# Down projections of a two-layer trunk: twelve instead of ten of 22 k-blocks in block products, the tiles reordered, square sums by transfers

## The chip, the cores and the metric

The kernel runs on one core of one Trainium2 chip. The metric is the device time of one execution in microseconds. TensorE (PE) multiplies matrices, VectorE (DVE) and ScalarE (ACT) do the elementwise work, SyncE (SP) and GpSimd (POOL) issue transfers; POOL also issues the transfers that add into their destination. Each engine runs its instructions in order and waits on semaphores for the others.

## The reference

Two layers over 512 positions of width 1024, float32. Layer 0 mixes with pooling and a gated short convolution, layer 1 with gated linear attention; each is followed by a gated convolution FFN of width 2816, and a final norm ends the trunk. The change concerns the last product of the FFN, `@ w_down`, and the sums of squares for the norms that follow it:

```
def rmsnorm(x, g):
    xf = x.astype(jnp.float32)
    y = xf * lax.rsqrt(jnp.mean(xf * xf, axis=-1, keepdims=True) + EPS)
    return (y * g.astype(jnp.float32)).astype(x.dtype)

def conv_ffn(h, w_up, conv_w, conv_b, w_down):
    u, v = jnp.split(h @ w_up, 2, axis=-1)
    u = causal_dwconv(u, conv_w, conv_b)
    return (jax.nn.gelu(u, approximate=False) * v) @ w_down

for l in range(DEPTH):
    ...
    x = x + y
    x = x + conv_ffn(rmsnorm(x, ffn_norm[l]), ffn_w_up[l], ffn_conv_w[l], ffn_conv_b[l], ffn_w_down[l])
return rmsnorm(x, final_norm)
```

## The kernel before

Channels lie on the 128 partitions, the 512 positions along a row. A float32 operand is split into a high part (rounded to the fast matmul type, by ScalarE) and a low part (the rest, by VectorE); every product is three passes: high by high, high by low, low by high.

**Down projection.** The 2816 inner channels are 22 k-blocks of 128, the output is eight tiles of 128 channels. Of the k-blocks, `NPLAIN` = 12 are multiplied plainly (`down`, two blocks of weights per tile as `DOWN_K` says). The other 10 are used in a scheme of Strassen and Winograd: the outputs are taken in four pairs of tiles (2p, 2p+1), the ten k-blocks as `HD` = 5 left and 5 right ones, the positions as two halves. In place of eight block products of 128 channels by 5 k-blocks by 256 positions there are seven, p1 to p7 (`DOWN_SEVEN` is their order), on sums of weights and sums of activations. `mix_m` forms and splits the activation sums for one left and one right k-block, HD times a layer; `down_seven` issues a pair's products and adds their results.

**Weights of a pair.** Four of the five k-blocks come by `seven_weights`. SP loads the left half (`raw 0`) and the right part (`raw 1`). The tile `s31` (tag "sum", `sums` buffers) is loaded by SP with a block twice over and then gets two more blocks added by a transfer that POOL issues (`add_sum`). From these VectorE makes s2 (`s2_sum`, L500, which reads s31 and raw 0) and s4 (`s4_sum`); ScalarE and VectorE split the pieces a1, s31p, s2 and a2 (L489, L495). The fifth k-block comes by `extra_weights`: three loads into `raw_e`, three VectorE sums (L548 to L550), one split (hi_e, lo_e). p1 and p2 use a1, p6 uses s2, p5 and p7 use s31p, p3 and p4 use a2; `seven_product` appends the extra block to each pass.

**Order.** Every step of TensorE, VectorE and ScalarE is entered with `at(t, ...)` and a planned time; `run_plan` sorts the entries and issues them, so each of these engines works in exactly that order. SP's and POOL's transfers are issued as their buffers and sources allow. The times `when` and `begin` in `seven_weights` are relative to the first product of the pair. Raw weights have three buffers (`wp`), split weights four of each kind (`wsp`), PSUM eight banks. The `dn` stage holds the "sum" buffers (two) and small ones.

Four whole plain tiles and tile 4 come first, then half of tile 5; behind each of the first three pairs stands one plain half tile, behind the last pair the whole of tile 7. After a pair, `done_left` and `done_right` add its tiles to x (`add_left`, `add_right`, `add_x`) and call `finish`, which squares the tile on ScalarE and adds it into a sum on VectorE (`square_acc`, L299). In the last layer tile 7 is done in two halves of positions, and `last` scales the first half and sends it out while the second is computed: `part` and `root` make the norm, `spread_small` spreads it, `scale_first` multiplies two tiles and sends them; `after(n, ...)` counts matmuls.

Of the kernel before, what the change touches and what calls it, by code (L numbers as in the profile page):

```python
# [14 lines left out]
P = 128  # L15
# [46 lines left out]
DOWN_LEFT = [NPLAIN + i for i in range(HK)] + [NF - 2]  # L62
DOWN_RIGHT = [NPLAIN + HK + i for i in range(HK)] + [NF - 1]
NDOWN = 6

COLS = {}
# [13 lines left out]
def trunk_kernel(ctx, tc, xT, cols, w_first, w_lead, w_ab, w_pool, w_abo, w_vg, w_qk, w_r, w_g2, w_go, w_up, w_dn, w_ds, w_de, out):  # L80
# [211 lines left out]

    def square_acc(k, acc, ts=slice(0, T)):
        if k == 0 and ts.start == 0:
            S.activation(acc[:, ts], x[0][:, ts], AF.Square)
            return
        sq = slot(name="sq")
        S.activation(sq[:, ts], x[k][:, ts], AF.Square)
        V.tensor_tensor(acc[:, ts], acc[:, ts], sq[:, ts], ALU.add)  # L299

# [160 lines left out]
    def seven_weights(src, base, pool, sums, behind=False, lead=None, later=0.0, begin=(26.0, 20.0, 15.4, 9.7), early=0.0):  # L461
# [73 lines left out]
    def extra_weights(src, base):  # L535

        e = {}

        def load():
            e["raw"] = wp.tile([P, WBLK], F32, tag="raw", name="raw_e")[:, : 7 * P]  # L540
            nc.sync.dma_start(e["raw"][:, : 2 * P], src[:, : 2 * P])
            e["r"] = e["raw"].rearrange("p (a n) -> p a n", n=P)
            nc.sync.dma_start(e["r"][:, 2:4, :], src[:, None, 2 * P : 3 * P].broadcast_to([P, 2, P]))
            nc.sync.dma_start(e["r"][:, 6, :], src[:, 3 * P :])

        def sums():
            r = e["r"]
            V.tensor_tensor(r[:, 2:4, :], r[:, 2:4, :], r[:, 0:7:6, :], ALU.add)  # L548
# [3 lines left out]
        def high():  # L552
            e["hi"] = wsp.tile([P, WPITCH], F32R, tag="hi", name="hi_e")[:, SKEW : SKEW + 7 * P]
            S.activation(e["hi"], e["raw"], AF.Copy)

        def low():
            e["lo"] = wsp.tile([P, WPITCH], F32R, tag="lo", name="lo_e")[:, SKEW : SKEW + 7 * P]
            V.tensor_tensor(e["lo"], e["raw"], f32(e["hi"]), ALU.subtract)

        at(base - 12.0, load)  # L560
        at(base - 7.0, sums)
        at(base - 3.0, high)
        at(base - 1.7, low)
        return e

    def seven_product(w, b, ops, name, out, first, ts, only=None, low_last=False, extra=None):
        if out not in b:
            b[out] = bank("st" + out)
        piece, side = LEFT[name]
        ks = [slice(side * QUARTER + k * P, side * QUARTER + (k + 1) * P) for k in range(HK)]  # L570
        h, lo = [[t[:, c] for c in ks] for t in w[piece]]
        if extra:
            c = (EXTRA_AT[piece] + side) * P
            h, lo = h + [extra["hi"][:, c : c + P]], lo + [extra["lo"][:, c : c + P]]
        ah, al = ops[name]()
        for i in range(3) if only is None else (only,):
            wt, a = ((h, ah), (lo, ah), (h, al))[i] if low_last else ((h, ah), (h, al), (lo, ah))[i]
            for k in range(len(a)):
                PE.matmul(  # L579
                    b[out][:, ts], wt[k], a[k],  # L580
                    start=first and i == 0 and k == 0, stop=i == 2 and k == len(a) - 1,
                    skip_group_check=True,
                )
# [73 lines left out]
    def ffn(l, acc, mixed, finish, ahead, halves_last=False):  # L657
# [223 lines left out]
        def plain_down(j, n=None):  # L881
            nonlocal t
            while blocks and n != 0 and (blocks[0][0] == j or (j == 0 and blocks[0][0] < 4)):
                jj, k0, kt = blocks.pop(0)
                n = n and n - 1
                first = t < base + 9.5 * UNIT
                block(t - 16.0, t - (9.3 if first else 6.0), t - (7.0 if first else 4.5))
# [11 lines left out]

        def done_left(p, late=0.0):  # L900
            at(t + late + 0.3, lambda: add_left(p))
            at(t + late + 2.3, lambda: finish(2 * p))

        def done_right(p, t):
            at(t, lambda: add_right(p))
            at(t + 2.4, lambda: finish(2 * p + 1))

        plain_down(0)
        plain_down(4)
        plain_down(5, 1)  # L910
        for p, (j, n) in enumerate(((5, 1), (6, 1), (6, 1), (7, 2))):
            sevens(p)
            done_left(p, 4.2 if n == 1 else 0.0)
            if p < HK - 1:
                done_right(p, t + 1.5 * n * NPLAIN * MM + 3.2)
            elif halves_last:
                at(t + 0.5, lambda: early_right(p))
            else:
                for i in range(KD - 2):
                    at(t + 0.5 + 1.3 * i, lambda i=i: pre_split(i, "mix1"))  # L920
            plain_down(j, n)
# [135 lines left out]
    def down_out(j):  # L1057
        if not total:
            total.append(slot(name="acc"))
        if j >= KD - 2:  # L1060
            pre_split(j, "mix1")
        square_acc(j, total[0])

# [463 lines left out]
    def last(j, half=None):  # L1527
# [3 lines left out]
        if half is None:  # L1531
            square_acc(j, acc)
            S.activation(x[j], x[j], AF.Copy, scale=col("fin", j))
# [27 lines left out]
        if half == 0:  # L1561
# [32 lines left out]
        for c in range(2):  # L1594
# [3 lines left out]
            for e in range(2):  # L1598
                queue = nc.scalar if c and e else nc.sync
                queue.dma_start(second_out[c * P : (c + 1) * P, e * T : (e + 1) * T], res[e])  # L1600

    def scale_first(ks):
# [89 lines left out]
```

## Time and profile before

| | |
|---|---|
| three runs | 998.9 us median, 997.78 to 999.17 |
| profiled execution | 998.05 us, span 996.3 us |
| granted TensorE clock | 0.998 |
| down projection, layer 0 | 349.88 to 462.95 us of the span |
| down projection, layer 1 | from 872.59 us to the end |

In the rows shown below PE is TensorE, PEld its weight load, DVE VectorE, ACT ScalarE. A group row gives line, engine, operation, output <- inputs and count. A timeline row begins with start and duration in us and ends, in brackets, with the idle time before it and what ended it. A row of waits gives who waited for whom: total us, times, longest. A row of transfers gives queue, count, size and us from issue to landing. Names: `s` is s31, `hi`/`lo` split weights, `sh`/`sl` those of s2, `raw` weights as loaded, `mh`/`ml` plain activations, `bh`/`bl`, `eh`/`el`, `xh`/`xl` split sums of activations, `kk` and `uu` the left and right results of a pair, `dn` and `st...` PSUM banks.

### The profile page before, as it was taken

The page shows a single profiled execution, that of the slowest core. Times are in us where ns is not written, and L with a number is a line of the kernel's source. Part 1 is how long each engine was busy: PE and PEld are TensorE (multiplying, and loading weights), DVE is VectorE, ACT ScalarE, POOL GpSimd, SP SyncE. Part 2 cuts the span into 40 slices and gives each one's busy share as a digit, 9 for nine tenths or more (in the row PEclk, how much of TensorE's full clock was granted, in tenths as well). Part 3 has the DMA queues.
Part 4 walks back from the last instruction along what each step waited for, and adds up shares of the span by engine and source line. Part 5 has one row for each costly group of instructions (what it writes and reads, how often), then busy time and mean ns, then how long its engine had stood idle before and what let it go on. Part 6 is the DMA issues. An engine that isn't in the chain of part 4 may idle for free.

```text
span 996.3 us, 18359 instructions
## 1 busy us (share of the span) xinstructions
PE 987.6 (99%) x7258; PEld 931.7 (94%) x7258; DVE 868.7 (87%) x1328; ACT 614.9 (62%) x1007; POOL 86.0 (9%) x109
## 2 busy tenths in 40 slices
PE   9999999999999999999999999999999999999997
PEld 7888889999999988999999999889999999988997
DVE  7886689999999998798779789889999999998795
ACT  6432467666766665445776566667776766665453
POOL 0000111111101000002000000111101101000000
PEclk9999999999999999999999999999999999999999
DMA  7423756778787454536335453767787787454532
GB/s 247 139 95 106 184 123 170 211 193 208 194 209 175 118 139 135 150 103 182 104 102 144 112 121 110 198 158 167 214 210 187 196 209 181 126 128 139 144 102 86
DMA packets 70327, 154.95 MB, mean 156 GB/s; under 512 B 5888, under 2 KB 11392, under 8 KB 70240
## 3 DMA queue, kind: packets, MB, share of 16 engines
q1 hardware_dynamic: 52192, 119.29, 36.9%
q0 software_dynamic: 17760, 34.08, 21.0%
q8 instruction: 57, 0.93, 0.4%
q10 hardware_dynamic: 288, 0.40, 0.1%
q14 instruction: 30, 0.25, 0.1%
HBM read 149.03 MB, written 2.10 MB: 152 GB/s over the span
## 4 chain that ended last, share of the span: by engine, by line
PE 97%; DVE 2%; DMA 0%; issue 0%; ACT 0%; DVEq 0%; ACTq 0%
PE stx L579 33%; PE styz L579 19%; PE dn L271 13%; PE go L271 4%; PE abo L271 4%; PE dn L579 3%; PE stz L579 2%; PE pu L963 2%; PE pc L271 2%; PE pb L271 2%; PE px L271 2%; PE vg L1171 2%; PE vg L1173 1%; PE vg L1172 1%; PE o L1262 1%; PE stw L579 1%
## 5 line engine op out<-in xcount | busy, mean ns | idle before, releaser
L495 DVE TENSOR_TENSOR lo<-raw,hi 128x1024 fp32r<-128x1024 f32 x120 | 146.2, 1219 | 16.4 <-ACT hi L489 16.2
L489 ACT ACTIVATE hi<-raw 128x1024 fp32r<-128x1024 f32 x120 | 125.7, 1058 | 27.8 <-PE styz L579 10.4
L471 POOL DMA_DIRECT2D s<-in_w_up x44 | 53.1, 1208 | 475.4 <-DVE v L1049 96.0
L226 ACT ACTIVATE hi<-raw 128x1024 fp32r<-128x1024 f32 (+3 forms) x69 | 64.7, 940 | 25.1 <-PE px L271 9.1
L230 DVE TENSOR_TENSOR lo<-raw,hi 128x1024 fp32r<-128x1024 f32 (+3 forms) x69 | 74.9, 1088 | 5.7 <-ACT hi L226 4.8
L364 DVE SCALAR_TENSOR_TENSOR cacc<-u,colt,cacc 128x511 f32<-128x511 f32 x96 | 71.4, 744 | 2.6 <-ACT cacc L361 2.5
L495 DVE TENSOR_TENSOR lo<-s,hi 128x1024 fp32r<-128x1024 f32 x60 | 73.0, 1216 | 0.0
L361 ACT ACTIVATE cacc<-u,colt 128x512 f32<-128x512 f32 x48 | 39.2, 816 | 42.8 <-DVE u L701 39.2
L579 PE MATMUL stx<-th,hi 128*128 128x256 f32 x416 | 64.5, 277 | 0.0
L579 PE MATMUL stx<-th,lo 128*128 128x256 f32 x416 | 64.1, 276 | 0.0
L579 PE MATMUL stx<-tl,hi 128*128 128x256 f32 x416 | 64.1, 276 | 0.0
L489 ACT ACTIVATE hi<-s 128x1024 fp32r<-128x1024 f32 x60 | 63.4, 1056 | 0.8
L579 PE MATMUL styz<-xh,lo 128*128 128x256 f32 x400 | 61.8, 276 | 0.7 <-DVE lo L495 0.7
L579 PE MATMUL styz<-xh,hi 128*128 128x256 f32 x400 | 62.0, 277 | 0.0
L579 PE MATMUL styz<-xl,hi 128*128 128x256 f32 x400 | 61.6, 276 | 0.0
L579 PEld LDWEIGHTS stx<-th,hi 128*128 128x128 f32 x416 | 54.9, 188 | 0.4 <-ACT n L1407 0.2
L579 PEld LDWEIGHTS stx<-tl,hi 128*128 128x128 f32 x416 | 54.9, 188 | 0.0
L579 PEld LDWEIGHTS stx<-th,lo 128*128 128x128 f32 x416 | 54.9, 188 | 0.0
L579 PEld LDWEIGHTS styz<-xh,lo 128*128 128x128 f32 x400 | 52.8, 188 | 0.9 <-DVE lo L495 0.9
L579 PEld LDWEIGHTS styz<-xh,hi 128*128 128x128 f32 x400 | 52.9, 188 | 0.0
L579 PEld LDWEIGHTS styz<-xl,hi 128*128 128x128 f32 x400 | 52.8, 188 | 0.0
L489 ACT ACTIVATE sh<-raw 128x512 fp32r<-128x512 f32 x60 | 37.9, 632 | 23.2 <-DVE raw L500 23.1
(387 smaller groups left out, 2635.7 us busy)
## 6 DMA issues: line engine op xcount, KB each, us to landing
s<-in_w_up SPq DMA_DIRECT2D x44, 512.0 KB, 6.9
s<-in_w_up POOLq DMA_DIRECT2D x44, 512.0 KB, 6.8
raw<-in_w_up SPq DMA_DIRECT2D x44, 512.0 KB, 6.5
raw<-in_w_dn SPq DMA_DIRECT2D x32, 384.0 KB, 3.1
raw<-in_w_up SPq DMA_DIRECT2D x44, 256.0 KB, 3.2
raw<-in_w_ab SPq DMA_DIRECT2D x12, 512.0 KB, 3.7
raw<-in_w_abo SPq DMA_DIRECT2D x8, 512.0 KB, 3.5
s<-in_w_ds SPq DMA_DIRECT2D x8, 512.0 KB, 5.8
```

The source lines that it names most:

```text
L226: S.activation(parts[0], raw, AF.Copy)
L230: V.tensor_tensor(parts[1], raw, f32(parts[0]), ALU.subtract)
L271: PE.matmul(out, w[:, k, :], a[k], start=first and i == 0 and k == 0, stop=last and i == 2 and k == n - 1, skip_group_check=loose,)
L361: S.activation(acc[0], u, AF.Identity, bias=col(bname, j), scale=col(wname, 2 * nj + j))
L364: V.scalar_tensor_tensor(a, u[:, : T - i], col(wname, (2 - i) * nj + j), a, ALU.mult, ALU.add)
L471: G.dma_start(w["s31"].rearrange("p (a n) -> p a n", a=2), part, accum_op=ALU.add)
L489: S.activation(h, src(), AF.Copy)
L495: V.tensor_tensor(lo, src(), f32(h), ALU.subtract)
L579: PE.matmul(b[out][:, ts], wt[k], a[k], start=first and i == 0 and k == 0, stop=i == 2 and k == len(a) - 1, skip_group_check=True,)
L963: PE.matmul(pus[g], parts[k][w][:, g * P : (g + 1) * P], a[k], start=k == 0 and i == 0, stop=k == KD - 1 and i == 2,)
L1171: PE.matmul(o[c][:, :n], xh[kk][:, cs], h[:, k, :], start=kk == 0, stop=False)
L1172: PE.matmul(o[c][:, :n], xl[kk][:, cs], h[:, k, :], start=False, stop=False)
```

## The change

Twelve k-blocks take part in the block products, ten stay plain (`HD` 6, `NPLAIN` 10, plain blocks of 5 and 5). Each pair has two extra k-blocks. Their s31 is no longer made on VectorE but by an adding transfer from POOL; the other sums and the right block lie in a new buffer `xe` (one of it), and there are two tiles of split extra weights with four splits in place of one. The "sum" buffers of the down stage go from two to one, and the begin and due times of a pair's weights change. Six whole plain tiles stand ahead of the first pair; one half of tile 6 stands behind pair 0, the other behind pair 1, nothing behind pair 2, tile 7 behind pair 3. A pair's left sum (`free_left`) is separated from the addition to x. The squares of tiles 1 to 5 are added by transfers from POOL (`queued`). In the last tile the spread norm is made later by matmul count, and tiles are scaled in the groups 0, 2 and 4, 6.

```diff
-HD = HK + 1
+HD = HK + 2
 NPLAIN = NF - 2 * HD
-DOWN_K = (6, 6)
-DOWN_AT = (0, 6)
+DOWN_K = (5, 5)
+DOWN_AT = (0, 5)
+EXTRA = 2 * P
 DOWN_UNIT = UNIT * HD / HK
-EXTRA_AT = {"a1": 0, "s31p": 2, "s2": 4, "a2": 5}
+EXTRA_AT = {"a1": (0, 0), "s31p": (0, 2), "s2": (1, 0), "a2": (1, 1)}
...
+MIXT = (19.6, 25.3, 31.0, 36.7, 42.4, 48.1)
+ET = (-16.0, -11.5, -9.0, -3.2, -1.7, 0.2, 0.9, 1.9, 5.3, 7.0)
...
-    def square_acc(k, acc, ts=slice(0, T)):
+    def square_acc(k, acc, ts=slice(0, T), queued=False):
...
-        V.tensor_tensor(acc[:, ts], acc[:, ts], sq[:, ts], ALU.add)
+        if queued:
+            G.dma_start(acc, sq, accum_op=ALU.add)
+        else:
+            V.tensor_tensor(acc[:, ts], acc[:, ts], sq[:, ts], ALU.add)
...
-            when = (-4.0, -2.9, 0.1, -2.6, -2.0, -0.7, -0.1, 2.5, 1.4, 4.5)
+            when = (-4.2, -2.9, -0.2, -4.0, -2.2, -0.5, 1.1, 4.3, 2.4, 5.8)
...
     def extra_weights(src, base):
 
         e = {}
+        blocks = src.rearrange("p (a n) -> p a n", a=4)
 
         def load():
...
+            raw = e["raw"] = wp.tile([P, WBLK], F32, tag="raw", name="raw_e")
+            nc.sync.dma_start(raw[:, : 2 * EXTRA], src[:, : 2 * EXTRA])
+            e["s31"] = raw[:, 2 * EXTRA :].rearrange("p (a n) -> p a n", a=2)
+            nc.sync.dma_start(e["s31"], blocks[:, 2:3, :].broadcast_to([P, 2, EXTRA]))
+
+        def add_sum():
+            G.dma_start(e["s31"], blocks[:, 0:4:3, :], accum_op=ALU.add)
+
+        def load_right():
+            e["xe"] = stage["dn"].tile([P, WBLK], F32, tag="xe", name="xe", bufs=1)[:, : 3 * EXTRA]
+            nc.sync.dma_start(e["xe"][:, 2 * EXTRA :], src[:, 3 * EXTRA :])
 
         def sums():
-            r = e["r"]
-            V.tensor_tensor(r[:, 2:4, :], r[:, 2:4, :], r[:, 0:7:6, :], ALU.add)
-            V.scalar_tensor_tensor(r[:, 4, :], r[:, 3, :], -1.0, r[:, 0, :], ALU.mult, ALU.subtract)
-            V.tensor_tensor(r[:, 5, :], r[:, 1, :], r[:, 4, :], ALU.subtract)
...
+            r, t = e["raw"], e["xe"]
+            V.scalar_tensor_tensor(t[:, :EXTRA], r[:, 3 * EXTRA :], -1.0, r[:, :EXTRA], ALU.mult, ALU.subtract)
+            V.tensor_tensor(t[:, EXTRA : 2 * EXTRA], r[:, EXTRA : 2 * EXTRA], t[:, :EXTRA], ALU.subtract)
...
-        at(base - 12.0, load)
-        at(base - 7.0, sums)
-        at(base - 3.0, high)
-        at(base - 1.7, low)
+        at(base + ET[0], load)
+        at(base + ET[1], add_sum)
+        at(base + ET[2], load_right)
+        at(base + ET[3], lambda: high(0, 0, WBLK))
+        at(base + ET[4], lambda: low(0, 0, WBLK))
+        at(base + ET[5], sums)
+        at(base + ET[6], lambda: high(1, 0, EXTRA))
+        at(base + ET[7], lambda: low(1, 0, EXTRA))
+        at(base + ET[8], lambda: high(1, EXTRA, 3 * EXTRA))
+        at(base + ET[9], lambda: low(1, EXTRA, 3 * EXTRA))
...
-        for t in (5.8, 6.6, 8.0, 10.3, 10.9, 11.5, 14.5, 15.2, 16.4, 17.6, 18.3, 19.0):
+        for t in (5.8, 6.6, 8.0, 10.3, 10.9, 14.5, 15.2, 16.4, 17.6, 18.3):
             at(base + t, split_m)
         for i in range(HD):
-            mix_m(i, base + 20.5 + 6.2 * i)
+            mix_m(i, base + MIXT[i])
...
-            w = seven_weights(w_ds[l, p], base, "dn", 2)
+            w = seven_weights(w_ds[l, p], base, "dn", 1, begin=(14.2, 10.6, 11.0, 6.2))
...
-        def add_left(p):
+        def free_left(p):
             kk = parts[p]["kk"]
             V.tensor_tensor(kk, o[2 * p], kk, ALU.add)
-            add_x(2 * p, kk)
...
-        def done_left(p, late=0.0):
-            at(t + late + 0.3, lambda: add_left(p))
-            at(t + late + 2.3, lambda: finish(2 * p))
+        def done_left(p, then):
+            at(t - 1.8, lambda: free_left(p))
+            at(then + (3.7 if p < HK - 1 else -1.1), lambda: add_x(2 * p, parts[p]["kk"]))
+            at(then + (5.7 if p < HK - 1 else 0.9), lambda: finish(2 * p))
...
-        plain_down(5, 1)
-        for p, (j, n) in enumerate(((5, 1), (6, 1), (6, 1), (7, 2))):
+        plain_down(5)
+        order = ((6, 1), (6, 1), (7, 0), (7, 2))
+        for p, (j, n) in enumerate(order):
             sevens(p)
-            done_left(p, 4.2 if n == 1 else 0.0)
+            gap = 1.5 * n * NPLAIN * MM if p < HK - 1 else 0.0
+            done_left(p, t + gap)
             if p < HK - 1:
-                done_right(p, t + 1.5 * n * NPLAIN * MM + 3.2)
+                done_right(p, t + gap + 7.8)
...
-                scale_first((0, 2))
-
-            after(14, both)
-            after(25, spread)
+                scale_first((0,))
+
+            after(17, both)
+            after(28, spread)
...
-        scale_first((4, 6))
+        scale_first((2, 4))
...
                 queue.dma_start(second_out[c * P : (c + 1) * P, e * T : (e + 1) * T], res[e])
+        scale_first((6,))
```

More of the change, by code (lines that the diff above doesn't have):

```diff
@@ new lines, in sums, with part @@
+        def sums():
+            r, t = e["raw"], e["xe"]
+            V.scalar_tensor_tensor(t[:, :EXTRA], r[:, 3 * EXTRA :], -1.0, r[:, :EXTRA], ALU.mult, ALU.subtract)
+            V.tensor_tensor(t[:, EXTRA : 2 * EXTRA], r[:, EXTRA : 2 * EXTRA], t[:, :EXTRA], ALU.subtract)
+        def part(kind, i, lo, hi):
+            if (kind, i) not in e:
+                e[kind, i] = wsp.tile([P, WPITCH], F32R, tag=kind, name=f"{kind}_e")[:, SKEW : SKEW + WBLK]
+            return e[kind, i][:, lo:hi], e["xe" if i else "raw"][:, lo:hi]
@@ new lines, in high, with low @@
+        def high(i, lo, hi):
+            h, raw = part("hi", i, lo, hi)
+            S.activation(h, raw, AF.Copy)
+        def low(i, lo, hi):
+            h = part("hi", i, lo, hi)[0]
+            low, raw = part("lo", i, lo, hi)
+            V.tensor_tensor(low, raw, f32(h), ALU.subtract)
+        at(base + ET[0], load)
[3 more added lines that the diff above has]
+        at(base + ET[4], lambda: low(0, 0, WBLK))
@@ L572, in seven_product @@
         if extra:
-            c = (EXTRA_AT[piece] + side) * P
-            h, lo = h + [extra["hi"][:, c : c + P]], lo + [extra["lo"][:, c : c + P]]
+            i, c = EXTRA_AT[piece]
+            ks = [slice((c + side) * EXTRA + k * P, (c + side) * EXTRA + (k + 1) * P) for k in range(HD - HK)]
+            h, lo = [x0 + [extra[e, i][:, c] for c in ks] for x0, e in ((h, "hi"), (lo, "lo"))]
         ah, al = ops[name]()
@@ L1531, in last @@
         if half is None:
-            square_acc(j, acc)
+            square_acc(j, acc, queued=j < KD - 2)
             S.activation(x[j], x[j], AF.Copy, scale=col("fin", j))
```

25 lines of the change are left out of this document (7 added, 18 removed).

## The prediction

> **What bounds the kernel now.** I read the page first (shares, then the chain that ended last), then who TensorE waited for, then busy time by stage in the first layer's down projection, then single rows.
>
> ```profile
> span 996.3 us, 18359 instructions
> PE 987.6 (99%) x7258; PEld 931.7 (94%) x7258; DVE 868.7 (87%) x1328; ACT 614.9 (62%) x1007; POOL 86.0 (9%) x109
> ...
> PE 97%; DVE 2%; DMA 0%; issue 0%; ACT 0%; DVEq 0%; ACTq 0%
> ```
>
> ```profile
> PE styz L579 <- DVE lo L495: 0.7, 1, 0.7
> ```
>
> ```profile
> 349.88:394.79 44.91, 44.91 (x200) 37.18 (x199) 42.25 (x75) 25.78 (x43) 2.41 (x2) 1.00 0.46 120
> 394.79:406.70 11.91, 11.91 (x106) 11.91 (x105) 6.09 (x10) 3.79 (x6) 1.20 (x1) 1.00 0.72 201
> 406.70:422.72 16.02, 16.02 (x125) 15.30 (x124) 12.62 (x19) 7.53 (x12) 1.20 (x1) 1.00 0.51 138
> ```
>
> TensorE sets the end: 97% of the chain, and beyond start-up the largest wait it has is 0.7 us. The windows (span of the stage, then PE, PEld, DVE, ACT, POOL busy, clock) are the 5.5 plain tiles, the first pair's seven products, and one plain half tile plus the second pair. TensorE never pauses in them, but VectorE is busy 42.25 of 44.91 us while it gets the first pair ready. So the change is worth what it takes off TensorE, less what makes TensorE wait for VectorE.
>
> **TensorE's own saving.** A 512-column matmul costs 1.36/6 = 0.2267 us by the step between these two rows (six matmuls each), a 256-column one 11.91/105 = 0.1134.
>
> ```profile
> 392.07 1.52 PE L271 MATMUL dn<-ml,hi 128*128 128x512 f32 x6
> 393.43 1.52 PE L271 MATMUL dn<-mh,lo 128*128 128x512 f32 x6
> ```
>
> Removed per layer: 8 tiles x 2 k-blocks x 3 passes x 0.2267 = 10.88 us. Added: 4 pairs x 7 products x 3 more matmuls x 0.1134 = 9.53. Saved: 1.35 us a layer, 2.7 in all, if TensorE never waits. A pair's products then take 126 x 0.1134 = 14.28 us, a plain half tile (5 k-blocks) 3.40. Pairs 0 to 1 and 1 to 2 start 17.68 us apart, but pair 3 starts 14.28 us after pair 2, because no plain work is left between them.
>
> **VectorE's prices**, as steps between rows with nothing waited for: 1024 wide 1.13 (duration 1.22), a 512-wide sum 0.61, 512 wide 0.60, 256 wide 0.34, dependent 256 wide 0.46, 768 wide 0.87; 640 wide, between 512 and 768, about 0.73 (estimate).
>
> ```profile
> 359.39 0.69 DVE L185 TENSOR_TENSOR ml<-cacc,mh 128x512 fp32r<-128x512 f32 x1 [0.68 <-ACT mh L184]
> 360.65 0.69 DVE L185 TENSOR_TENSOR ml<-cacc,mh 128x512 fp32r<-128x512 f32 x1 [0.57 <-ACT mh L184]
> ...
> 363.99 0.42 DVE L757 TENSOR_TENSOR cacc<-cacc 128x256 f32<-128x256 f32 x1
> 364.45 0.43 DVE L758 TENSOR_TENSOR cacc<-cacc 128x256 f32<-128x256 f32 x1
> ...
> 389.01 0.42 DVE L548 TENSOR_TENSOR raw_e<-raw_e 128x256 f32<-128x256 f32 x1
> ...
> 390.00 1.22 DVE L495 TENSOR_TENSOR lo<-raw,hi 128x1024 fp32r<-128x1024 f32 x1
> 391.13 0.68 DVE L500 SCALAR_TENSOR_TENSOR raw<-s,raw 128x512 f32<-128x512 f32 x1
> 391.74 1.08 DVE L558 TENSOR_TENSOR lo_e<-raw_e,hi_e 128x896 fp32r<-128x896 f32 x1
> ...
> 401.87 0.42 DVE L845 TENSOR_TENSOR kk<-stz,kk 128x256 f32<-128x256 f32 x1 [2.58 <-PE stz L579]
> 402.21 0.95 DVE L230 TENSOR_TENSOR lo<-raw,hi 128x768 fp32r<-128x768 f32 x1
> 403.08 0.42 DVE L548 TENSOR_TENSOR raw_e<-raw_e 128x256 f32<-128x256 f32 x1
> ...
> 429.71 0.69 DVE L299 TENSOR_TENSOR acc<-acc,sq 128x512 f32<-128x512 f32 x1
> 430.31 0.69 DVE L868 TENSOR_TENSOR uu<-dn,uu 128x512 f32<-128x512 f32 x1
> ```
>
> **First pair.** It starts at 349.88 + 6 x 6.80 = 390.68, 4.1 us earlier than now. VectorE's low part of piece a1 (L495) runs now at 390.00. Ahead of it the change takes away two splits of m (1.20) with the two waits shown (1.25), the old sums of the extra weights (0.99), and changes ten 768-wide lows into eleven 640-wide ones (-0.67). It puts ahead of it the sixth mix_m (0.34 + 0.60 + 4 x 0.46) and s2_sum (0.61), 3.39 together. That gives 389.28, or 1.40 before the pair. The new lo_e follows and ends 0.95 after the pair's start. TensorE needs it at 1.81 (p1's third pass begins after 12 matmuls, the extra blocks are its fifth and sixth). No stall. But the rest queues up behind: ta and tb lows 1.20, s2 low 0.60, two sums 0.92, s4_sum 0.60, extra low 0.34, so the low part of s31p, planned for +2.4, starts at x = -1.40 + 2 x 1.13 + 3.66 = +4.5.
>
> **The s31 buffer: where I expect the loss.** The "sum" buffers go from two to one (`seven_weights(..., "dn", 1, ...)`). A pair's s31 may be loaded only when the pair before has done with its own, and the last reader is that low part. What must follow, one after the other, is the load on SP, the adding transfer on POOL, and s2_sum on VectorE at pair - 4.0. With two buffers none of this was near TensorE's path.
>
> ```profile
> 412.56 1.22 DVE L495 TENSOR_TENSOR lo<-s,hi 128x1024 fp32r<-128x1024 f32 x1
> ...
> 413.80 0.38 SPq L467 DMA_DIRECT2D s<-in_w_ds  x1
> ...
> 417.85 0.46 SPq L544 DMA_DIRECT2D raw_e<-in_w_de  x1
> ...
> 419.48 1.20 POOL L471 DMA_DIRECT2D s<-in_w_ds  x1 [17.20 <-DVE lo L230]
> 420.64 0.43 DVE L548 TENSOR_TENSOR raw_e<-raw_e 128x256 f32<-128x256 f32 x1 [1.53 <-DMA raw_e<-in_w_de]
> ```
>
> ```profile
> raw_e<-in_w_de SPq DMA_DIRECT2D x1, 64.0 KB, 2.7
> ...
> s<-in_w_ds POOLq DMA_DIRECT2D x1, 512.0 KB, 5.6
> ...
> s<-in_w_ds POOLq DMA_DIRECT2D x1, 512.0 KB, 6.1
> ...
> s<-in_w_ds POOLq DMA_DIRECT2D x1, 512.0 KB, 5.5
> ...
> s<-in_w_ds POOLq DMA_DIRECT2D x1, 512.0 KB, 6.7
> ```
>
> Even now a load starts 0.02 us after such a low part ends (413.78 to 413.80), for the pair after next. Load issue to adding transfer: 5.68. The adding transfer lands 5.5 to 6.7 after its issue (four rows). A landed transfer reaches VectorE in 0.09 (417.85 + 2.7 to 420.64). Sum C = 0.02 + 5.68 + 5.6 + 0.09 = 11.4, taking the lower middle row for the adding transfer, because the 6.1 began 0.3 us after a weight load and the new one starts well behind it; bounds 11.3 and 12.5.
>
> VectorE works in order: behind a waiting s2_sum stand a1's low part and lo_e, for which TensorE waits, and in the last pair also a 256-wide add to uu (0.34) and kk's sum (0.60).
>
> - Pair 1: s2_sum at 4.5 + 1.22 + 11.39 - 17.68 = -0.57; lo_e ends 0.61 + 1.13 + 1.22 = 2.96 later, at 2.39; needed at 1.81: stall 0.58. After a stall lo_e ends at 1.81, so x becomes 0.59 + 1.13 + 0.60 + 0.92 + 0.60 + 0.34 = 4.18.
> - Pair 2: -0.89, lo_e at 2.07, stall 0.26, x again 4.18.
> - Pair 3: 4.18 + 12.61 - 14.28 = 2.51; lo_e 3.90 later, at 6.41: stall 4.60.
>
> Together 5.44 a layer; less the saving, 4.09; two layers +8.2 us. Bounds: with C = 12.5, stalls 1.68, 1.36 and 5.70, less 1.35, twice: +14.8. With VectorE on plan (x = 2.4) and C = 11.3 only the last pair stalls, 2.72: +2.7.
>
> The Trainium skill (DMA: Bandwidth & Descriptors, Anatomy of one DMA) fits a transfer from POOL's queue as 2.0 us plus its bytes over 436 GB/s, 3.2 us for 512 KB. The four rows, at 5.5 to 6.7, do not agree; by that figure for both transfers C would be about 6.5 (an estimate) and nothing would stall, the second rival's case.
>
> **The rest.** ScalarE gets two more splits of the extra weights and one 128 wider; it is busy 7.53 of 16.02 us, so it hides them, and without that cover they would cost, at VectorE's prices for these widths, 0.34 + 0.60 + 0.13 = 1.1 us a pair. The extra weights' loads stay three SP issues a pair, plus one adding transfer of 256 KB on POOL. This shape is not in the trace; the 512 KB rows bound it above at 6.7 and 64 KB's 2.7 below, and its due time is 8.3 us ahead of its reader. A waiting s31 load holds SP's later loads, which have over 6 us to their readers. The five square sums a layer that leave VectorE free 3.0 us where nothing waits for it. As transfers they stand in POOL's queue.
>
> At the end the spread row scaling comes nearer to the last matmul.
>
> ```profile
> 985.32 0.60 PE L337 MATMUL bc<-ident,y 128*128 128x128 f32 x4
> 985.68 0.83 PE L271 MATMUL dn<-ml,hi 128*128 128x256 f32 x5
> 985.96 1.28 DVE L1606 TENSOR_TENSOR xall<-xall,bc 128x512 f32<-128x512 f32 x2 [0.99 <-PE bc L337]
> 986.35 0.87 PE L271 MATMUL dn<-mh,lo 128*128 128x256 f32 x6
> ...
> 987.26 0.43 DVE L858 TENSOR_TENSOR dn<-dn,rs 128x256 f32<-128x256 f32 x1
> ...
> 990.30 1.41 DVE L1597 TENSOR_SCALAR res<-to,y 128x512 f32<-128x512 f32 x2
> 990.94 1.34 SPq L1600 DMA_DIRECT2D out<-res  x3
> ```
>
> The transposes come two matmuls before the end: one scaling (0.64) starts 0.05 after the last matmul (-0.23 - 0.36 + 0.64) and holds VectorE to 0.69, where L858 came at 0.2: +0.5. The scaling of tiles 6 and 7 now follows the two res (991.71 + 0.5 + 0.64), so the last output goes out at 992.8 in place of 991.8: +1.0, between 0 (hidden by the other outputs) and 1.1.
>
> Sum against the profiled execution (998.05 us, 0.85 below the median, 1.75 above its span): 998.05 + 8.2 + 1.0 = 1007.2.
>
> **Rivals.**
> 1. *Only the last pair stalls.* VectorE reaches s31p's low part on plan and the transfers are quick: 998.05 + 2.7 + 0 = 1000.8. For it: pairs 1 and 2 stall by only 0.3 to 0.6 above. Against: the first pair's preparation is 2 us late.
> 2. *Faster.* The last pair stalls only if 2.4 + 1.22 + C - 14.28 + 3.90 exceeds 1.81, so from C = 8.6 (6.8 with x = 4.18). If the two transfers together stay below that, or the buffer is handed over sooner than I read it, TensorE's saving stands: 998.05 - 2.7 + 1.0 = 996.3. For it: nothing in the stage waits now. Against: the fastest rows sum to 11.3.
> 3. *POOL's queue takes over.* Each square transfer must land before the next one into the same accumulator.
>
> ```profile
> POOL acc L626 <- DMA acc<-sq: 15.0, 3, 7.5
> ```
>
>    POOL is in order. One such wait (mean 5.0 us of the three, longest 7.5) ahead of the last pair's adding transfer would be added whole in both layers: 1007.2 + 10 to 15, 1017 to 1022. Against: the adding transfer is due some 4 us ahead of the square of that stretch.
> 4. *No change*: stalls of about 1.35 us a layer, C near 9.9 with x = 2.4: about 999.
>
> **How the numbers follow.** A clear difference here is 0.2%, 2 us. Forecast (1003 to 1012) 0.47; rival 1 (999.9 to 1003) 0.18; rival 3 0.09; rival 2 0.20; rival 4 0.06. Faster 0.20, same 0.06, slower 0.74. The likeliest case's own range is 1001 to 1014; with most of rival 2 it is 996 to 1014.
>
> **What would show it.** The profile after should have a wait of VectorE's s2_sum (L500's successor) for the adding transfer, and TensorE's first product of pair 3 idle 3 to 6 us for lo_e in each layer, with under 1 us at pairs 1 and 2 and none at pair 0. Matmul steps unchanged, 126 of them a pair. The s31 load should start within 0.1 us of the low part of s31p. If TensorE does not pause at pair 3, the buffer's chain is wrong and the time is near 996; if POOL waits for a square's landing ahead of an adding transfer, rival 3 is right.

## The result and the profile after

The changed kernel takes 1019.99 us in the median of five runs (1019.03 to 1021.71) against 998.72 for the kernel before, measured beside it (997.78 to 999.17): a ratio of 1.0216, 95% interval 1.0201 to 1.0231, so 21.3 us slower. The forecast was 1007.2 us: the right side, and 12.8 us too little. The profiled execution has a span of 1018.9 us, 22.6 more than before.

The page of the changed kernel (shares and chain of waits), then its waits (who waited for whom: total us, times, longest):

```profile
span 1018.9 us, 18635 instructions
PE 993.5 (98%) x7324; PEld 939.0 (92%) x7324; DVE 869.3 (85%) x1338; ACT 622.6 (61%) x1027; POOL 104.9 (10%) x127
...
PE 83%; DVE 7%; DMA 6%; issue 1%; ACT 1%; DVEq 0%; POOL 0%; POOLq 0%; ACTq 0%; SPq 0%
```

```profile
PE stx L604 <- ACT uu L867: 6.7, 2, 4.0
PE stx L604 <- DVE lo L501: 6.3, 4, 2.4
PE stx L604 <- DVE lo_e L576: 2.2, 4, 1.0
...
DVE raw L506 <- DMA s<-in_w_ds: 35.7, 6, 7.5
...
ACT uu L867 <- DMA acc<-sq: 9.5, 2, 5.4
```

TensorE's share of the chain falls from 97% to 83%; VectorE and transfers take its place. s2_sum (now L506) waits for s31's adding transfer six times, once for each pair but the first of a layer, for 35.7 us in all; TensorE waits in those pairs for a1's low part (lo), for lo_e, and for uu, whose copy in turn waits for a square's transfer (acc<-sq), which the forecast did not have.

Busy time by stage: pairs 0 to 3 of layer 0, then pairs 1 to 3 of layer 1 (span of the stage, then PE, PEld, DVE, ACT, POOL busy, granted clock, DMA share, GB/s):

```profile
390.44:404.73 14.29, 14.29 (x127) 14.29 (x126) 9.61 (x15) 5.34 (x10) 2.22 (x2) 1.00 0.66 168
...
408.16:427.46 19.30, 16.53 (x127) 16.12 (x126) 13.60 (x20) 7.57 (x12) 3.34 (x3) 0.91 0.57 142
...
430.89:453.70 22.81, 17.00 (x127) 16.41 (x126) 14.16 (x21) 9.24 (x14) 4.25 (x4) 0.88 0.63 149
453.70:468.65 14.95, 14.95 (x127) 14.95 (x127) 13.76 (x22) 7.90 (x14) 1.72 (x2) 0.96 0.50 124
```

```profile
944.21:963.13 18.92, 16.51 (x127) 16.10 (x126) 13.60 (x20) 8.91 (x14) 3.31 (x3) 0.91 0.64 159
...
966.56:983.81 17.25, 14.57 (x127) 14.37 (x126) 10.10 (x17) 8.05 (x13) 4.24 (x4) 1.00 0.73 176
983.81:1000.35 16.54, 14.98 (x128) 14.52 (x127) 16.18 (x25) 8.77 (x16) 1.75 (x2) 1.00 0.35 80
```

Pair 0 takes 14.29 us, as forecast, with nothing waited for. The six later pairs take 24.0 us more than 6 x 14.29. Span less PE busy is idle: 2.77, 5.81, 0, 2.41, 2.68 and 1.56, together 15.2 us. PE busy less 14.29 is 2.24, 2.71, 0.66, 2.22, 0.28 and 0.69, together 8.8 us: the same 126 matmuls at a granted clock of 0.88 to 0.96, or restarted after a wait. These are the places where the time went, not yet its cause: a slow stretch ahead of a later wait shortens that wait (point 4 below). Against the spans: 24.0 lost, 2.7 of TensorE's work saved, 1.1 added behind the last matmul, 22.4 of the 22.6.

The chain of s31 (the steps that follow one another from the last use of its buffer to the next s2_sum) in the first layer, from the low part of pair 0's s31p to pair 1's products, in one timeline:

```profile
394.84 1.22 DVE L501 TENSOR_TENSOR lo<-s,hi 128x1024 fp32r<-128x1024 f32 x1
...
396.13 0.38 SPq L473 DMA_DIRECT2D s<-in_w_ds  x1
...
399.62 1.20 POOL L553 DMA_DIRECT2D raw_e<-in_w_de  x1 [14.95 <-DVE kk L870]
403.71 1.21 POOL L477 DMA_DIRECT2D s<-in_w_ds  x1 [2.89 <-DVE kk L888]
...
410.19 0.69 DVE L506 SCALAR_TENSOR_TENSOR raw<-s,raw 128x512 f32<-128x512 f32 x1 [6.61 <-DMA s<-in_w_ds]
410.80 1.22 DVE L501 TENSOR_TENSOR lo<-raw,hi 128x1024 fp32r<-128x1024 f32 x1
411.94 1.22 DVE L576 TENSOR_TENSOR lo_e<-raw_e,hi_e 128x1024 fp32r<-128x1024 f32 x1
...
412.07 0.74 PE L604 MATMUL stx<-bh,lo 128*128 128x256 f32 x4 [2.38 <-DVE lo L501]
413.21 0.50 PE L604 MATMUL stx<-bh,lo_e 128*128 128x256 f32 x2 [0.40 <-DVE lo_e L576]
```

The load starts 0.07 us after the low part ends (394.84 + 1.22 = 396.06), the adding transfer follows 7.58 us later, s2_sum 6.48 us after that: 14.1 us where the sum had 11.4. a1's low part starts only behind s2_sum. The leg from load to adding transfer, in the kernel before (5.68 us, the leg that the sum used) and here:

```profile
413.80:419.48 5.68, 5.68 (x53) 5.68 (x52) 5.08 (x7) 2.43 (x4) 0.00 (x0) 1.00 0.53 172
```

```profile
396.13:403.71 7.58, 7.58 (x69) 7.58 (x68) 3.95 (x6) 1.72 (x4) 1.20 (x1) 1.00 0.96 246
```

The transfer engines are busy for 0.96 of this leg, against 0.53 before: raw 0, the extra weights with their adding transfer, and from 401.62 raw 1 are now loaded beside s31.

And uu, near the end of pair 2: the square's transfer on POOL, ScalarE's copy to uu, and TensorE's product p4 behind it:

```profile
441.35 1.44 POOL L303 DMA_DIRECT2D acc<-sq  x1
...
449.26 0.38 ACT L867 ACTIVATE uu<-stx 128x256 f32<-128x256 f32 x1 [5.40 <-DMA acc<-sq]
...
449.69 1.23 PE L604 MATMUL stx<-xh,hi 128*128 128x256 f32 x4 [4.04 <-ACT uu L867]
```

uu takes a slot that a squared tile still holds, and that tile is let go when its transfer has landed: uu's copy starts 7.9 us after the transfer's issue.

### The profile page after: what moved, and what is told of

Same layout as the page of the kernel before. It is cut to its first block, busy times and chain, and to the rows that moved or that the text cites. A ratio compares the mean times of both kernels' runs of the same rounds, so it can differ in the third digit from the quotient of the medians.

```text
span 1018.9 us, 18635 instructions
## 1 busy us (share of the span) xinstructions
PE 993.5 (98%) x7324; PEld 939.0 (92%) x7324; DVE 869.3 (85%) x1338; ACT 622.6 (61%) x1027; POOL 104.9 (10%) x127
## 4 chain that ended last, share of the span: by engine, by line
PE 83%; DVE 7%; DMA 6%; issue 1%; ACT 1%; DVEq 0%; POOL 0%; POOLq 0%; ACTq 0%; SPq 0%
PE stx L604 31%; PE styz L604 19%; PE dn L274 5%; PE go L274 4%; PE abo L274 4%; DMA s<-in_w_ds 3%; PE pu L990 2%; PE pc L274 2%; PE pb L274 2%; PE px L274 2%; PE stz L604 2%; PE dn L604 2%; PE vg L1198 1%; PE vg L1200 1%; PE vg L1199 1%
## 5 line engine op out<-in xcount | busy, mean ns | idle before, releaser
L495 ACT ACTIVATE hi<-raw 128x1024 fp32r<-128x1024 f32 x120 | 125.9, 1059 | 42.2 <-PE styz L604 11.4
L229 ACT ACTIVATE hi<-raw 128x1024 fp32r<-128x1024 f32 (+3 forms) x69 | 61.4, 892 | 43.9 <-PE stx L604 15.6
L233 DVE TENSOR_TENSOR lo<-raw,hi 128x1024 fp32r<-128x1024 f32 (+3 forms) x69 | 70.2, 1021 | 14.8 <-ACT hi L229 14.1
L506 DVE SCALAR_TENSOR_TENSOR raw<-s,raw 128x512 f32<-128x512 f32 x60 | 41.1, 685 | 35.7 <-DMA s<-in_w_ds 35.7
```

Source lines behind the costliest of these rows:

```text
L229: S.activation(parts[0], raw, AF.Copy)
L233: V.tensor_tensor(parts[1], raw, f32(parts[0]), ALU.subtract)
L495: S.activation(h, src(), AF.Copy)
L506: V.scalar_tensor_tensor(s2, w["s31"][:, QUARTER:], -1.0, w["raw", 0][:, :QUARTER], ALU.mult, ALU.subtract)
```

## The experiments

Three theories were set against each other. A: the single s31 buffer makes a chain, and VectorE's order (s2_sum ahead of a1's low part and lo_e) carries it to TensorE. B: the squares' transfers slow the chain and hold slots. A third one came up on the way: the order in which POOL and the weight buffers serve the transfers. Each ratio below is to the kernel before, measured beside that run (medians of 998.07 to 998.64 us).

**e1_squares_dve: the squares back on VectorE.**

```diff
-        square_acc(j, total[0], queued=j < KD - 2)
+        square_acc(j, total[0])
```

The same in `last`.

> The changed kernel with the sums of squares back on VectorE; everything else stays. Theory A (the single s31 buffer: a chain from the low part of s31p over load and adding transfer to s2_sum, which stands ahead of a1's low part and lo_e in VectorE's order): the chain stays at 13 to 15 us in pairs 1 and 2, their idle of TensorE stays at 2 to 3 us each, uu's wait on acc<-sq (9.5 us in all) goes, but then pair 3 shows a wait for lo_e of its own, 4 to 6 us a layer: 1012 to 1020 in all. Theory B (the squares' transfers make the chain long, in POOL's queue and on the transfer engines, and hold uu's slot): the chain falls to the 11.4 us of the forecast and the whole lands near the forecast, 1003 to 1009.

Measured: 1024.65 us, ratio 1.0270 (1.0252 to 1.0288), slower still and 4.7 us above the range of theory A. Pair 3 of layer 0, in TensorE's timeline and in the stages:

```profile
452.66 0.96 PE L604 MATMUL stx<-bh,lo 128*128 128x256 f32 x4 [5.00 <-DVE lo L501]
454.40 0.80 PE L604 MATMUL stx<-bh,lo_e 128*128 128x256 f32 x2 [0.77 <-DVE lo_e L576]
```

```profile
446.15:469.52 23.37, 17.61 (x129) 17.11 (x127) 17.94 (x28) 9.24 (x16) 0.00 (x0) 0.85 0.31 81
```

uu's wait is gone, and pair 3 now waits 5.77 us at lo and lo_e (4.55 in layer 1), where the prediction had 4.60. The chain, worked out like the one above for six pairs, takes 13.2 us in the mean (12.1 to 14.2) against 13.5 (12.5 to 15.3) in the changed kernel. So the squares' transfers are not what makes it long, and B falls as the main cause. The two waits hide each other: while TensorE waits for uu in pair 2, the chain of pair 3 runs on. Behind pair 3's wait the clock falls (0.85 in the row above), and no later wait hides it: PE is busy for 3.3 us more than 14.29 there, and for 2.7 more in pair 3 of layer 1.

**e2_s2_late: s2_sum behind a1's low part and lo_e.**

```diff
-            when = (-4.2, -2.9, -0.2, -4.0, -2.2, -0.5, 1.1, 4.3, 2.4, 5.8)
+            when = (-4.2, -2.9, -0.2, 0.5, 1.0, 2.2, 2.1, 4.3, 2.4, 5.8)
```

Here s4_sum comes ahead of s2's low part, and both use one tile, so that low part is made from the later sum. This kernel computes something else than the reference, and only its time is of use; the instructions and their number are the same.

> The changed kernel with s2_sum, s2's high and low part and s4_sum planned later (0.5, 1.0, 2.2 and 2.1 us after the pair's start in place of -4.0, -2.2, -0.5 and 1.1), so that a1's low part and lo_e stand ahead of s2_sum in VectorE's order. Theory A: the idle of TensorE at lo and lo_e goes in pairs 1 and 2, with the low clock behind it (5.0 and 6.6 us in layer 0); what stays is uu's wait on a square's transfer, and in pair 3 a late s2 (its plain gap is missing): 1002 to 1010. Theory B: transfers that are slow because of the squares still hold uu and now s2 itself: 1014 to 1020, with TensorE's waits moved from lo_e to s2's parts.

Measured: 1007.34 us, ratio 1.0088 (1.0070 to 1.0107); 12.7 us of the loss are gone. TensorE's waits:

```profile
PE stx L604 <- ACT uu L867: 3.9, 2, 2.0
PE stx L604 <- ACT kk L867: 3.6, 5, 1.7
```

No wait for lo or lo_e is left, and the granted clock is 1.00 in all pairs. What stays is uu, and a new wait for kk: ScalarE stands at s2's high part, which waits for s2_sum, ahead of the copy to kk. This is as A has it: the order on VectorE carries the chain to TensorE. But the gain is that of a kernel with s4_sum too early; e12 below has the same order with s4_sum behind s2's low part, and loses the gain again.

**e3_before_queued: the kernel before with squares by transfers.** The edit brings `queued` into that kernel:

```diff
-        V.tensor_tensor(acc[:, ts], acc[:, ts], sq[:, ts], ALU.add)
+        if queued:
+            G.dma_start(acc, sq, accum_op=ALU.add)
+        else:
+            V.tensor_tensor(acc[:, ts], acc[:, ts], sq[:, ts], ALU.add)
...
-        square_acc(j, total[0])
+        square_acc(j, total[0], queued=j < KD - 2)
```

> The kernel before with one edit: five of the seven whole sums of squares of each layer's down projection are adding transfers on POOL's queue. Theory A: they cost nothing where s31 has two buffers: 997 to 1000. Theory B: they delay the s31 transfers and hold slots here too: 1003 or more, with TensorE's wait for uu or lo_e in the trace.

Measured: 998.69 us, ratio 1.0005 (0.9996 to 1.0015), and none of the waits of TensorE above. With two s31 buffers and that kernel's slots the squares' transfers cost nothing, as the prediction had it.

**e4_before_one_sum: the kernel before with one s31 buffer.**

```diff
-            w = seven_weights(w_ds[l, p], base, "dn", 2)
+            w = seven_weights(w_ds[l, p], base, "dn", 1, begin=(14.2, 10.6, 11.0, 6.2))
```

> The kernel before with one edit: one s31 buffer in the down projection, with the changed kernel's due times for its four transfers. Here s2_sum stands behind a1's low part, pairs are 16.0 us apart and s31p's low part starts 1.8 us into a pair. Theory A, with the chain at 13 to 15 us whatever the squares do: s2_sum comes 0 to 2 us into the next pair, lo_e 0 to 2 us late for TensorE in three pairs a layer: 999 to 1008. Theory B, with the chain at 11.4 us without squares' transfers: s2_sum 1.4 us ahead of the pair, nothing waits: 998 to 1000.

Measured: 1006.38 us, ratio 1.0082 (1.0067 to 1.0097). One buffer with its due times costs 8.3 us, without any other part of the change. (The edit also moves the loads of raw 0 and raw 1 from 15.4 and 9.7 us ahead of the pair to 11.0 and 6.2.) The last pair of layer 0:

```profile
432.74 0.38 SPq L467 DMA_DIRECT2D s<-in_w_ds  x1
...
437.10 1.20 POOL L471 DMA_DIRECT2D s<-in_w_ds  x1 [17.56 <-DVE acc L299]
...
446.00 0.69 DVE L500 SCALAR_TENSOR_TENSOR raw<-s,raw 128x512 f32<-128x512 f32 x1 [3.87 <-DMA s<-in_w_ds]
...
447.75 0.39 PE L579 MATMUL stx<-bh,lo_e 128*128 128x256 f32 x1 [2.91 <-DVE lo_e L558]
```

Here the chain takes 13.3 us (low part's end 432.71 to 446.00) and 12.2 in the mean of six. The leg from load to adding transfer is 4.9 us in the mean, against 6.4 in the changed kernel, and from there to s2_sum 7.2 against 7.0. So the adding transfer is slow here too, without squares' transfers and without one for the extra weights. That the whole costs less than in the changed kernel fits three differences, none of which was tried alone: a1's low part stands ahead of s2_sum, all pairs are 16.0 us apart, and no transfer for the extra weights stands ahead of s31's on POOL.

**e5_two_sums: the changed kernel with two s31 buffers.** To make room, the extra weights' second part lies in two 256-wide tiles (`t`, `right`) in place of `xe`; its split is in three pieces instead of two.

```diff
-            w = seven_weights(w_ds[l, p], base, "dn", 1, begin=(14.2, 10.6, 11.0, 6.2))
+            w = seven_weights(w_ds[l, p], base, "dn", 2, begin=(22.0, 17.0, 11.0, 6.2))
...
-            e["xe"] = stage["dn"].tile([P, WBLK], F32, tag="xe", name="xe", bufs=1)[:, : 3 * EXTRA]
-            nc.sync.dma_start(e["xe"][:, 2 * EXTRA :], src[:, 3 * EXTRA :])
+            e["right"] = half("xr")
+            nc.sync.dma_start(e["right"], src[:, 3 * EXTRA :])
```

> The changed kernel with two s31 buffers (loads due 22 and 17 us ahead of the pair); to make room the extra weights' second part lies in two small tiles in place of xe, which costs one more high part and one more low part of 256 columns a pair. Theory A (the single buffer is the cause): VectorE no longer waits for the adding transfer ahead of a1's low part, no idle of TensorE at lo or lo_e, and TensorE's saving of 2.7 us stands against 1.0 at the end: 996 to 999; uu's wait on a square's transfer may stay, 2 to 4 us a layer, then 999 to 1004. Rival: the stage is short of VectorE time or of transfer capacity whatever the buffer; then TensorE still idles at lo_e in pairs 1 to 3 and the time is 1008 or more.

Measured: 1000.54 us, ratio 1.0036 (1.0014 to 1.0059). Pairs 1 and 2 of layer 0, and what is left in pair 2:

```profile
408.24:422.53 14.29, 14.29 (x127) 14.29 (x126) 12.98 (x21) 7.25 (x13) 3.37 (x3) 1.00 0.72 187
...
425.96:441.82 15.86, 14.60 (x128) 14.41 (x126) 11.22 (x19) 7.07 (x13) 3.00 (x3) 1.00 0.62 142
```

```profile
439.63 0.74 PE L609 MATMUL stx<-xh,hi 128*128 128x256 f32 x4 [1.26 <-ACT uu L872]
```

No wait for lo or lo_e, pair 1 at its 14.29 us and full clock; uu's slot costs 1.26 and 1.45 us. In layer 1 pair 1 also waits 0.73 us for hi_e.

**e6_two_sums_j3: the square of tile 3 on VectorE.** e5 with, at both calls of `square_acc`:

```diff
-queued=j < KD - 2)
+queued=j < KD - 2 and j != 3)
```

> As e5_two_sums, with the square of tile 3 (the one whose slot uu of pair 2 waits for) back on VectorE. If uu's wait is a matter of that one slot, uu no longer waits on acc<-sq and this is 1 to 4 us faster than e5_two_sums: 995 to 999. If the slots are short in general, another tile's transfer takes its place and the two are equal.

Measured: 1004.26 us, ratio 1.0047 (1.0030 to 1.0065), not told apart from e5_two_sums, since the intervals overlap; uu still waits 1.52 and 1.15 us. The wrong tile had been named: the transfers that remain ahead of pair 2's end are those of tiles 1 and 2.

**e7_half_between: a plain half tile between every two pairs.**

```diff
-        plain_down(5)
-        order = ((6, 1), (6, 1), (7, 0), (7, 2))
+        plain_down(5, 1)
+        order = ((5, 1), (6, 1), (6, 1), (7, 2))
```

> The changed kernel with 5.5 plain tiles ahead of the first pair and a plain half tile between every two pairs, as before the change; everything else stays. Theory A: pair 3 now starts 17.7 us after pair 2, so its share of the chain's delay falls from 4 to 6 us to the 2 to 3 of pairs 1 and 2; pair 0 starts 3.4 us sooner and waits up to 2 us for its own lo_e: 1012 to 1018. If the missing gap were the main cost: 1005 or less. If only uu's wait counts: unchanged, 1018 to 1022.

Measured: 1023.36 us, ratio 1.0255 (1.0222 to 1.0288). Theory A missed by 5 us: its range ended at 1018. The four runs spread from 1019.60 to 1030.39, and the profile is of the fastest. uu no longer waits and pair 2 takes its 14.3 us, but pair 1 waits 2.54 us at lo, pair 3 1.66, and pair 0, 3.6 us earlier, takes 17.0 us in place of 14.3. The missing half tile is not the cause; it only decides in which pair the delay shows.

**e8_one_sum_plan: one buffer, the plan arranged around it.** One buffer, with the edit of e7, the line shown for e6, and:

```diff
-            when = (-4.2, -2.9, -0.2, -4.0, -2.2, -0.5, 1.1, 4.3, 2.4, 5.8)
+            when = (-4.2, -2.9, -0.2, 0.25, 2.3, 3.0, 3.1, 4.3, 0.6, 5.8)
```

> One s31 buffer as in the changed kernel, with the plan arranged around it: s2_sum behind a1's low part and lo_e, s2's high part behind the copy to kk, s31p's low part 1.8 us sooner, a plain half tile between every two pairs, the square of tile 3 on VectorE. Theory A with a chain of 13 to 15 us: s31p's low part starts 1 to 3 us into a pair, the chain ends 1 us before to 1.5 us after the next pair's start, and s2 is needed only 4.1 us after it: no idle in the pairs: 996 to 1000. If the low clock or ScalarE's order adds waits of its own: 1002 to 1010.

Measured: 1032.77 us, ratio 1.0354 (1.0325 to 1.0384), the slowest of all and far above both ranges. Pair 2 of layer 0 takes 25.5 us:

```profile
431.29 0.80 PE L604 MATMUL stx<-bh,hi_e 128*128 128x256 f32 x2 [2.78 <-ACT hi_e L571]
...
450.09 0.74 PE L604 MATMUL stx<-xh,hi 128*128 128x256 f32 x4 [3.90 <-ACT uu L867]
```

The chain no longer waits at lo; the extra weights' high part (hi_e) and uu's slot do, each behind its own transfer.

**e9_two_sums_q345: two buffers, squares of tiles 1 and 2 on VectorE.** e5 with, at both calls of `square_acc`:

```diff
-queued=j < KD - 2)
+queued=2 < j < KD - 2)
```

> As e5_two_sums, but the squares of tiles 1 and 2, whose slots kk and uu of pair 2 wait for, are back on VectorE; tiles 3, 4 and 5 stay as transfers. If the last idle of e5_two_sums (1.26 and 1.45 us at uu) comes from those two slots, it goes, and the time is 2 to 3 us below e5_two_sums: 995.5 to 998. If VectorE has no room for two more sums in pairs 1 and 2, or another square's slot takes their place: 999 to 1002.

Measured: 996.94 us (996.30 to 998.29), ratio 0.9988 (0.9979 to 0.9996): 1.4 us faster than the kernel before by the medians, less than the 2 us that the prediction called a clear difference. Pairs 1 to 3 of layer 0:

```profile
408.43:422.72 14.29, 14.29 (x127) 14.29 (x126) 13.61 (x22) 7.28 (x13) 2.43 (x2) 1.00 0.73 189
...
426.15:440.44 14.29, 14.29 (x127) 14.29 (x126) 13.45 (x22) 7.97 (x14) 2.11 (x2) 1.00 0.52 138
440.44:454.72 14.28, 14.28 (x128) 14.28 (x127) 12.55 (x22) 8.22 (x16) 1.72 (x2) 1.00 0.55 132
```

TensorE does not pause in any pair. The span of the profiled execution, the fastest of the eleven, is 994.6 us, 1.7 below the one before: the saving of 2.7 less the 1.0 at the end, the two terms as the prediction had them.

**e10_two_sums_dve: two buffers, no square as a transfer.** e5 with, at both calls of `square_acc`:

```diff
-, queued=j < KD - 2)
+)
```

> As e5_two_sums with no square as a transfer. If the squares' transfers cost only through the slots they hold, and VectorE has room once it does not wait for s31: 995.5 to 998, uu's wait gone. If VectorE is the bound of the last two pairs, the five sums (3.4 us a layer) show as idle of TensorE: 1001 to 1006.

Measured: 996.95 us, ratio 0.9987 (0.9976 to 0.9998), as e9. With two buffers VectorE has room for all seven sums; the squares by transfers bring nothing here.

**e11_small_tiles_one_sum: the control of e5.** e5 with:

```diff
-            w = seven_weights(w_ds[l, p], base, "dn", 2, begin=(22.0, 17.0, 11.0, 6.2))
+            w = seven_weights(w_ds[l, p], base, "dn", 1, begin=(14.2, 10.6, 11.0, 6.2))
```

> The control of e5_two_sums: its two small tiles in place of xe, but one s31 buffer and the changed kernel's due times. Theory A (the buffer): the chain and the idle at lo and lo_e are back, 1016 to 1024. If the rearranged extra weights had made the difference: 1000 to 1004.

Measured: 1027.11 us, ratio 1.0286 (1.0273 to 1.0299), 3 us above theory A's range. The rearranged tiles alone gain nothing; they cost 7 us against the changed kernel, and the 26.6 us between this and e5 are the second buffer with its earlier due times.

**e12_s2_late_2: s2_sum late, and its high part behind the copy to kk.**

```diff
-            when = (-4.2, -2.9, -0.2, -4.0, -2.2, -0.5, 1.1, 4.3, 2.4, 5.8)
+            when = (-4.2, -2.9, -0.2, 0.5, 2.3, 2.9, 3.0, 4.3, 2.4, 5.8)
```

> The changed kernel, one s31 buffer, with s2_sum 0.5 us, s2's high part 2.3, its low part 2.9 and s4_sum 3.0 us after the pair's start: behind a1's low part and lo_e on VectorE as in e2_s2_late, and now also behind the copy to kk on ScalarE. Theory A: no idle at lo or lo_e; ScalarE's wait for s2_sum no longer holds the copy to kk; what stays is uu's slot and a late s2 in pair 3: 1002 to 1008. If the order on VectorE is not the point: 1015 or more.

Measured: 1025.54 us, ratio 1.0277 (1.0259 to 1.0294), far above the 1002 to 1008 of theory A. s4_sum and SP's and POOL's transfers for pair 1, and TensorE's waits:

```profile
396.93 0.38 SPq L473 DMA_DIRECT2D s<-in_w_ds  x1
...
397.51 0.69 DVE L512 TENSOR_TENSOR raw<-raw 128x512 f32<-128x512 f32 x1
...
398.23 0.33 SPq L548 DMA_DIRECT2D raw_e<-in_w_de  x1
...
402.15 1.20 POOL L477 DMA_DIRECT2D s<-in_w_ds  x1 [15.02 <-DMA raw_e<-in_w_de]
403.66 1.20 POOL L553 DMA_DIRECT2D raw_e<-in_w_de  x1 [0.31 <-DVE lo L233]
```

```profile
PE stx L604 <- ACT hi_e L571: 17.6, 6, 4.8
```

The same two rows in the changed kernel:

```profile
393.91 0.69 DVE L512 TENSOR_TENSOR raw<-raw 128x512 f32<-128x512 f32 x1
...
394.62 0.33 SPq L548 DMA_DIRECT2D raw_e<-in_w_de  x1
```

lo and lo_e no longer wait for s2_sum, as intended. But s4_sum is the last reader of a weight buffer, and the extra weights' load takes that buffer 0.03 us after it ends (398.20 to 398.23; 394.60 to 394.62 in the changed kernel). With s4_sum behind s31p's low part the load falls behind s31's, on POOL too: the extra weights are added 4.0 us later than the 399.62 of the changed kernel, and hi_e is late in the place of lo. e2 had s4_sum ahead of that low part (end 396.15, load 396.18) and kept the good order. In pair 3 here the extra weights are added first, and hi_e is late all the same: ScalarE stands ahead of it at a square, 5.81 us, for another square's transfer. So the third theory is a part of the picture: with one s31 buffer the delay moves from one buffer to the next, and A's fix by order works only while the others stay in time.

## Why the prediction was right in kind and too small

1. **TensorE's saving** (1.35 us a layer, 14.28 a pair): right. Pair 0 and every undisturbed pair take 14.28 to 14.29; e9 shows the saving in the span.
2. **The first pair**: right. It starts at 390.44 (390.68 forecast), without a stall, and s31p's low part 4.40 us into it (4.5).
3. **The buffer**: right as a mechanism, shown by e5 against e11 and, in the kernel before, by e4. **The mis-sized term is C**, from the end of s31p's low part to the next s2_sum. The prediction had 11.4 us, at most 12.5; the six chains of the changed kernel take 13.5 in the mean. Load to adding transfer was 6.4 in place of 5.68, adding transfer to s2_sum 7.0 in place of 5.7. Pricing the refill by rows that had slack was the step that failed. The trace before had slower ones: of its eight adding transfers of this size in the two down stages the sum used four, and the second one in each stage, issued 2.0 and 1.9 us behind another, took 8.2 and 8.1 us to land. With 8.2 the upper bound of C would have been 14.0.

   This term is nearly the whole gap. The prediction's own formula with the six measured chains gives delays of 3.2, 4.1 and 6.2 us in layer 0 and 2.8, 1.3 and 5.7 in layer 1, 23.3 in all, where 24.0 were lost; 998.05 + 23.3 - 2.7 + 1.0 = 1019.65, and the profiled execution took 1020.6. For pair 1 of layer 0, with its 14.13, it puts s2_sum at 4.40 + 1.22 + 14.13 - 17.72 = 2.03 and lo_e's first use 3.2 us late; measured 3.24 (413.21 against 408.16 + 1.81).

   Why the refill took longer is in part argued. The rows of before came from a stage where s31 was fetched well ahead; with one buffer and the new due times its transfers fall together with those of the extra weights, of raw 0 and of raw 1 (the 0.96 against 0.53 above). In e4, without an adding transfer for the extra weights, the chain takes 12.2; in e1, with it, 13.2; with the squares' as well, 13.5, within the spread of the six. No run takes this traffic away and leaves the single buffer.
4. **What had no term: the clock.** After several of the waits TensorE runs at about half its rate for some us, which is most of the 8.8 us of PE busy beyond 14.29 a pair. Every forecast idle was priced at its own length. But this explains little of the miss. The transfers and VectorE set when the next s2_sum comes: from s2_sum to s31p's next low part VectorE takes 5.22 us in pairs 1 and 2 of both layers, whether the clock fell in that pair or not. So slow matmuls ahead of a later wait only shorten that wait. What counts is the slow stretch behind the last wait: PE busy beyond 14.29 in pair 3 is 0.66 and 0.69 us here, against 3.3 and 2.7 in e1.
5. **The squares at nothing**: half right. On the kernel before they cost nothing (e3). In the changed kernel "nothing waits for it" failed: a squared tile's slot is uu's next one, and p4 waited 4.04 and 2.68 us for it. But this was no added loss. Without it (e1) pair 3 waits for the buffer instead, as forecast, and the whole is 4.7 us slower. Once the buffer is doubled, the slot is what remains: 3.6 us from e5 to e9.
6. **Where the stalls fall.** The forecast had 0.58, 0.26 and 4.60 us in pairs 1, 2 and 3; pairs 1 and 2 had 2.8 and 1.8 at lo and lo_e in layer 0, and pair 3 none, since uu's wait in pair 2 had given its chain time; in layer 1 they had 2.4, none and 1.6. So the sign that the prediction named, 3 to 6 us of idle at pair 3 and under 1 us at pairs 1 and 2, did not show in either layer; e1, without uu's wait, has it at pair 3. The idle of all pairs is 15.2 us where 10.9 were forecast, and with the slow stretches 24.0.
7. **The end**: right. From the start of tile 7 to the end of the span, less tile 7's own matmuls, it is 1.1 us longer (1.0 forecast), and the last output is, as forecast, that of the scaling that now follows the two res (`scale_first((6,))`).

Of the rivals, the third named the time (1017 to 1022) but not the mechanism: no adding transfer waited for a square to land ahead of it on POOL; the square held a slot. The second, faster, is what the change gives with two buffers and the squares of tiles 1 and 2, or all of them, back on VectorE: it named 996.3, e9 and e10 have 996.94 and 996.95. By the rule of the Trainium skill that spoke for it (DMA: Bandwidth & Descriptors, Anatomy of one DMA: 3.2 us for 512 KB) nothing would have stalled; the adding transfers here took 6.1 to 8.2 us to s2_sum.

## What to carry to other kernels

When a buffer is taken away, time its refill from the traffic that will then stand beside it, not from rows taken when it was fetched early, and look at what stands behind its reader on an in-order engine. A wait that is removed may only have hidden the next one, so a part of a change is judged with the other parts in place: doubling the buffer was worth 20 us, while moving squares, steps or plain work around the single one cost 3 to 13 us more in every kernel that computes the reference (e1, e7, e8, e12). When TensorE waits on a chain that the other engines and the transfers set, work out that chain first: slow matmuls between two such waits cost little, those behind the last one cost their full length.

## What the runs showed of the hardware

The clock after an idle depends on more than the length of the idle. Granted clock (third number from the end of a row) in 5 us from the restart, for the changed kernel after its uu wait of 4.04 us, and after its wait of 0.41 us in pair 2 that followed one of 1.36:

```profile
449.69:454.69 5.00, 5.00 (x23) 5.00 (x24) 3.40 (x5) 3.38 (x5) 0.90 (x1) 0.50 0.41 72
434.92:439.92 5.00, 5.00 (x43) 5.00 (x44) 4.93 (x9) 2.49 (x5) 0.00 (x0) 1.00 0.45 147
```

The same for e1, after an idle of 1.88 us in layer 0 and of 1.86 in layer 1, and for e4 after 2.91 us:

```profile
411.79:416.79 5.00, 4.90 (x27) 4.61 (x28) 4.97 (x8) 2.08 (x5) 0.00 (x0) 0.66 0.26 75
947.96:952.96 5.00, 4.59 (x37) 4.39 (x38) 4.97 (x8) 2.70 (x5) 0.00 (x0) 1.00 0.28 86
```

```profile
447.75:452.75 5.00, 5.00 (x44) 5.00 (x45) 4.90 (x8) 2.46 (x5) 0.00 (x0) 1.00 0.55 157
```

Two idles of nearly the same length, in the same place of the two layers, end one at 0.66 and one at full clock, and a longer one leaves it alone. The Trainium skill (TensorE: Matmul & The Clock Gate, Part 1: The HAM clock gate) has the clock halved after an idle window of about 3.4 us and calls the window free-running, so that the outcome may differ from run to run. The trace agrees with the half rate, and two outcomes for nearly equal idles fit a free-running window; it does not agree that the idle must last 3.4 us, since 1.88 us were once enough.
